# A hybrid decoder trunk: the compressed branch's second products moved behind query tiles, the Ln/Exp table load moved behind the last SiLU, and six of the last eight output tiles computed by halves of the tokens

## The chip, the cores and the metric

The kernel runs on one core of one Trainium2 chip. The metric is the device time of one execution in microseconds (us), smaller is better; it is measured for the whole program, from its start to the landing of its last output. A profiled execution gives the trace; its span runs from the first instruction to the last.

## The reference, cut to what matters

The program is a two-layer decoder trunk on 512 tokens of width 1024, in float32. Layer 0 has a recurrent mixer, layer 1 a sparse-attention mixer; each layer then has a SwiGLU feed-forward block, and a last RMSNorm makes the output. Three pieces matter here:

```python
def compress_blocks(k, pos_emb, w1, w2):
    ...
    return jax.nn.silu(flat @ w1) @ w2

def swiglu(h, w_gate_up, w_down):
    g, u = jnp.split(h @ w_gate_up, 2, axis=-1)
    return (jax.nn.silu(g) * u) @ w_down

h = h + swiglu(rmsnorm(h, ffn_norm[layer]), w_gate_up[layer], w_down[layer])
...
return rmsnorm(h, final_norm)
```

`compress_blocks` is applied to the keys and to the values of one attention branch: a first product with w1, a SiLU, and a small second product with w2 (64 by 64).

## The kernel before

**Layout.** Activations lie transposed: eight tiles of 128 features by 512 tokens (`h[0]` to `h[7]`). Each float32 operand of a product is split in a high part (a cast on ScalarE, L78) and a low part (a subtraction on VectorE, or on GpSimd for the query weights, L79), and one product takes three matmuls (L89, L90, L91). There are seven buffers for such pairs of weights (`wh`, `wl`) and three for raw weights.

**Order of the work.** The program is written as straight Python. A scheduler then orders the instructions of each engine by a simulated clock, with the order in the text as the priority; every engine runs its list in that order and waits at an instruction whose inputs are not there. An instruction with no inputs can float forward unless an edge pins it. `keep_in_program_order` pins an instruction behind the last instruction written before it on its engine. `issue_after(x)`, which the change uses more, pins what is written in its block on x's engine behind x, in the order of issue only.

**Activation tables.** ScalarE's Ln and Exp can share one table set, which L168 loads at the start and L355 is to load again at the end of each feed-forward block; SiLU (L343) has a set of its own. The toolchain inserts a load wherever the set that is active lacks the function. When it inserts loads for Ln and Exp by itself, each gets its own set.

**The odd mixer (`odd`, L703).** Four projections (L720), the row norm `row_rstd` (L735, with Ln at L127 and Exp at L128), then for each projection a tile `z` (L740). The first two go to `compress` (L825): copies into `cx` (L832), the first product (L837, eight fp32 matmuls), a SiLU made of `sigmoid` (L149: Exp, Ln, Exp) and VectorE steps that end in `u` (L850), and the second product `ps_c2` (L853 for the keys, L858 for the values). The values and gates of all tokens (`ps_v`, L755) follow, and then four query tiles (`query_tile`, L784, `AHEAD` = 4) of 24 matmuls each, before the attention loop. So in the text the second products come ahead of `ps_v` and of the query tiles. `w2` lies in the pool `oe`, which closes before the query tiles.

**The feed-forward block (`ffn`, L270).** The gate and up projections use a seven-product scheme (`product`, L290, tile `p`), the hidden tiles `hh`, `hl` (L347, L348) feed the down projection `ps_d` (L309). The row norm of the block is made in the first round, at L333. L355 stands behind the loop, but its pin goes to the last ScalarE instruction written, a weight cast of L309.

**The end (`finish`, L363).** Hidden tiles 18 to 21 are multiplied with the last weights. Output tiles 0 to 5 are made whole (L368 to L373), each squared and added to `acc`; tiles 6 and 7 by halves of the tokens (256 columns each). For each half, `pn` (L387, L389) sums the squares over the features, `rstd` (L123) makes the norm, and eight products with it (L397, L399), on VectorE and GpSimd, make the output, which goes out in four stores (L400). The first half's `acc` holds tiles 0 to 5 over all tokens.

Of the kernel before, what the change touches and what calls it, by code (L numbers as in the profile page):

```python
# [9 lines left out]
F32 = mybir.dt.float32  # L10
# [3 lines left out]
ALU = mybir.AluOpType  # L14
# [3 lines left out]
P = 128  # L18
# [16 lines left out]
BANK_OUT = (0, 3)  # L35
OWN_DOWN = (0, 3, 6)
AHEAD = 4
LEVELS = (16, 8, 4, 2, 1)
# [14 lines left out]
class Core:  # L53
# [68 lines left out]

    def rstd(self, ps, n, out):  # L123

        nc = self.nc
        t = self.sp.tile([P, T], F32, tag="tmp", name="rt", bufs=2)[:, :ps.shape[1]]
        nc.scalar.activation(t, ps, AF.Ln, bias=self.eps, scale=1.0 / n)  # L127
        nc.scalar.activation(out, t, AF.Exp, scale=-0.5)  # L128
        nc.vector.scalar_tensor_tensor(t, out, -0.5 / n, out, ALU.mult, ALU.mult)
        nc.vector.scalar_tensor_tensor(t, ps, n * EPS, t, ALU.add, ALU.mult)  # L130
        nc.vector.scalar_tensor_tensor(out, t, 1.5, out, ALU.add, ALU.mult)

# [137 lines left out]
    def ffn(self, outs, w_out, gain, layer, next_gain):  # L270
        tc, nc, io, sp = self.tc, self.nc, self.io, self.sp
        with tc.tile_pool(name="fs", bufs=1) as fs, tc.tile_pool(name="fps", bufs=6, space=PSUM) as fps:
# [44 lines left out]
            for size in GROUPS:  # L317
                hid = []
                for j in range(done, done + size):
# [22 lines left out]
                    (nc.vector if j == NF - 1 else nc.gpsimd).tensor_tensor(g, g, r, ALU.mult)  # L342
                    nc.scalar.activation(g, g, AF.Silu)  # L343
                    nc.vector.tensor_tensor(g, s, g, ALU.mult)
# [9 lines left out]
                done += size  # L354
            tc.keep_in_program_order(nc.scalar.preload_act_table_set("natural_log_exp_and_others"))  # L355
            if next_gain is None:
# [6 lines left out]
    def finish(self, hid, ws, fps):  # L363

        nc, fs, sp, h = self.nc, self.fs, self.sp, self.h
        gain = lambda m: self.par[:, C_GAIN + 32 + m:C_GAIN + 33 + m]
        acc = sp.tile([P, T], F32, tag="acc", name="acc", bufs=1)
        for m in range(KD - 2):  # L368
            ps = self.bank(m, "ps_d")
            self.dense_t(ps, self.weight(ws[m]), hid)  # L370
            nc.vector.tensor_tensor(h[m], ps, h[m], ALU.add)
            self.square(m, h[m], acc)
            nc.scalar.activation(h[m], h[m], AF.Identity, scale=gain(m))  # L373
        w = [self.weight(ws[m]) for m in (KD - 2, KD - 1)]
        for half in range(2):
            c = slice(half * TH, (half + 1) * TH)
            pn = fps.tile([P, T], F32, tag="gu", name="pn")[:, :TH]
            sqs = []
            for i in range(2):
                m = KD - 2 + i  # L380
                ps = fps.tile([P, T], F32, tag="gu", name="ps_f")[:, :TH]
                self.dense_t(ps, w[i], [(xh[:, c], xl[:, c]) for xh, xl in hid])
                nc.vector.tensor_tensor(h[m][:, c], ps, h[m][:, c], ALU.add)
                sq = fs.tile([P, TH], F32, tag="u", name="sq", bufs=4)
                nc.scalar.activation(sq, h[m][:, c], AF.Square)
                sqs.append(sq)
            nc.tensor.matmul(pn, self.ones, acc[:, c], start=True, stop=False)  # L387
            for i, sq in enumerate(sqs):
                nc.tensor.matmul(pn, self.ones, sq, start=False, stop=i == 1)  # L389
            r = fs.tile([P, TH], F32, tag="tr", name="r", bufs=7)  # L390
            self.rstd(pn, D, r)
            for i in (0, 2, 3, 1):
                o = fs.tile([P, 2, TH], F32, tag="sw" if half else ("g", "s")[i // 2], name="o", bufs=4 if half else 2)
                for j in range(2):
                    m = 2 * i + j
                    if i == 3:
                        nc.vector.scalar_tensor_tensor(o[:, j], h[m][:, c], gain(m), r, ALU.mult, ALU.mult)  # L397
                    else:
                        (nc.gpsimd if i == 2 or (i == 1 and j) else nc.vector).tensor_tensor(o[:, j], h[m][:, c], r, ALU.mult)  # L399
                nc.sync.dma_start(self.io["out"][2 * i:2 * i + 2, :, c].rearrange("m p t -> p m t"), o)  # L400
# [302 lines left out]
    def odd(self, xs, acc):  # L703
        tc, nc, io, sp = self.tc, self.nc, self.io, self.sp
        with tc.tile_pool(name="os", bufs=1) as os_, tc.tile_pool(name="ops", bufs=2, space=PSUM) as op:
# [20 lines left out]
            with tc.tile_pool(name="oe", bufs=1) as oe:  # L726
                self.oe = oe
                w1 = [oe.tile([P, 8, P], F32, tag="w1", name="w1", bufs=2) for _ in range(2)]
                w2 = oe.tile([64, 2, 64], F32, name="w2")
                for i in range(2):  # L730
# [5 lines left out]
                pss += [proj(2), proj(3)]  # L736
                rt = self.token_rstd(r, op.tile([P, T], F32, tag="po", name="ps_rt", bufs=1))
                for col, ps in enumerate(pss):
                    z = oe.tile([P, T], F32, tag="z", name="z", bufs=3)
                    nc.vector.tensor_tensor(z, ps, r, ALU.mult)  # L740
                    if col < 2:
                        self.compress(col == 1, z, w1[col], w2, kc, vc)
                    else:
                        for g in range(2):
                            self.keys(z, g, *[a[:, col - 2] for a in kk[g]])
# [27 lines left out]
            with tc.tile_pool(name="ol", bufs=1) as ol_:  # L773
# [10 lines left out]
                def query_tile(step, late=True):  # L784

                    raw = raws.popleft()
                    w = self.split(raw, WN, True)
                    query_load()
                    yield
                    ps = self.bank(0, "ps_q") if late else op.tile([P, T], F32, tag="pt", name="ps_q", bufs=3)  # L790
                    for k, (xh, xl) in enumerate(xs):
                        wh, wl = w[k // 4]
                        c = slice(k % 4 * P, k % 4 * P + P)
                        self.mm3(ps, wh[:, c], wl[:, c], xh, xl, k == 0, k == 7)
                        if k % step == step - 1:
                            yield
                    z = ol_.tile([P, T], F32, tag="qz", name="qz", bufs=9)
                    nc.vector.scalar_tensor_tensor(z, ps, 0.125, r, ALU.mult, ALU.mult)
                    qz.append(z)
                    yield  # L800

                for _ in range(2):
                    query_load()
                for _ in range(AHEAD):
                    for _ in query_tile(1, False):
                        pass
                self.attention(qz, outs, kk, kc, vt, vc, v3, gates, query_tile)
                for i, o in enumerate(outs):
# [15 lines left out]

    def compress(self, is_v, z, w1, w2, kc, vc):  # L825
        nc, os_, op = self.nc, self.os, self.op
# [12 lines left out]
        pc = os_.tile([64, 1], F32, tag="cpc", name="cpc", bufs=1)  # L839
        u = os_.tile([64, 2, 31], F32, tag="cu", name="cu", bufs=1)  # L840
        e = os_.tile([64, 2, 31], F32, tag="ce", name="ce", bufs=1)
# [7 lines left out]
        self.sigmoid(s, n, e)  # L849
        nc.vector.tensor_tensor(u, u, s, ALU.mult)  # L850
        ps2 = op.tile([P, T], F32, tag="pt", name="ps_c2", bufs=3)
        if not is_v:
# [308 lines left out]
```

## Time and profile before

| what | value |
|---|---|
| median of 3 runs | 1310.82 us (1310.17 to 1310.92) |
| the profiled execution's own time | 1311.86 us |
| its span, first to last instruction | 1308.9 us |
| TensorE busy | 1270.2 us, 97% of the span |
| TensorE's mean granted clock | 0.984 of full |
| ScalarE table loads | 21, 1.283 us each |

The profiled execution is 1.04 us above the median, and 2.96 us of its time lie outside the span. [...]

### The profile page before, as it was taken

Reading aid. Unit: us, or ns where it says so; the run is one execution under the profiler, and the core shown is the slowest. Engines: PE = TensorE matmul, PEld = TensorE weight load, DVE = VectorE, ACT = ScalarE, POOL = GpSimd, SP = SyncE. Lnnn points to the kernel's source line nnn. Section 1 sums busy time; section 2 is a strip of 40 time slices with the busy share of each in tenths; the row PEclk is TensorE's granted clock in tenths of the full one; section 3 lists DMA queues with packets and bytes.
Section 4 is the critical chain, followed back from the end, with each engine's and each line's share of the span. In section 5 each row is a group of like instructions: output and inputs, shape, how many; then the busy total and the mean of one; then the engine's idle time right before and its main releaser. Section 6 shows DMA issues by size and latency. Waiting matters only on the chain.

```text
span 1308.9 us, 21707 instructions
## 1 busy us (share of the span) xinstructions
PE 1270.2 (97%) x7846; PEld 1120.7 (86%) x7846; DVE 1028.2 (79%) x2027; ACT 731.7 (56%) x1587; POOL 332.0 (25%) x371
## 2 busy tenths in 40 slices
PE   9999999998999999999988999999989999999995
PEld 7888888888999999999877888887889999999984
DVE  7896764699998887876762789995989888878755
ACT  6655444675554444444554778895755444444444
POOL 3432431001121111111015666762012111111101
PEclk9999999999999999999997999999989999999998
DMA  7212212123233333332322211101223333333321
GB/s 262 84 65 75 72 65 65 65 81 101 85 109 109 107 106 100 100 97 88 104 90 93 78 52 52 44 18 34 85 81 125 105 97 98 97 101 102 105 57 64
DMA packets 44123, 115.10 MB, mean 88 GB/s; under 512 B 4913, under 2 KB 10481, under 8 KB 44017
## 3 DMA queue, kind: packets, MB, share of 16 engines
q1 hardware_dynamic: 43872, 113.69, 27.2%
q8 instruction: 61, 1.00, 0.3%
q14 instruction: 46, 0.37, 0.1%
q10 hardware_dynamic: 144, 0.04, 0.0%
HBM read 111.62 MB, written 2.10 MB: 87 GB/s over the span
## 4 chain that ended last, share of the span: by engine, by line
PE 60%; DVE 8%; issue 2%; DMA 2%; ACT 2%; POOL 1%; DVEq 0%; ACTq 0%; POOLq 0%
PE p L89 9%; PE p L90 9%; PE p L91 9%; PE ps_d L90 5%; PE ps_d L91 5%; PE ps_d L89 5%; DMA raw<-in_gu 2%; PE po L966 2%; PE pt L935 2%; PE ps_o L89 2%; PE ps_o L91 2%; PE ps_o L90 2%; DVE wl L79 1%; PE ps_q L89 1%; PE ps_q L90 1%
## 5 line engine op out<-in xcount | busy, mean ns | idle before, releaser
L78 ACT CAST wh<-raw 128x512 fp32r<-128x512 f32 (+2 forms) x356 | 212.8, 605 | 216.2 <-PE p L90 76.8
L79 DVE TENSOR_TENSOR wl<-raw,wh 128x512 fp32r<-128x512 f32 (+2 forms) x340 | 244.0, 723 | 43.2 <-ACT wh L78 42.1
L214 ACT CAST sh<-sw 128x512 fp32r<-128x512 f32 x176 | 107.6, 618 | 144.4 <-PE p L90 126.4
L341 POOL TENSOR_TENSOR s<-s,rstd 128x256 f32<-128x256 f32 x44 | 38.9, 884 | 510.9 <-DVE s L336 451.7
L215 DVE TENSOR_TENSOR sl<-sw,sh 128x512 fp32r<-128x512 f32 x176 | 146.3, 848 | 6.5 <-ACT sh L214 6.2
L90 PE MATMUL ps_d<-hl,wh 128*128 128x512 f32 x344 | 136.0, 395 | 0.4 <-DVE hl L348 0.2
L91 PE MATMUL ps_d<-hh,wl 128*128 128x512 f32 x344 | 135.6, 394 | 0.0
L89 PE MATMUL ps_d<-hh,wh 128*128 128x512 f32 x344 | 134.5, 396 | 0.6 <-ACT hh L347 0.5
L342 POOL TENSOR_TENSOR g<-g,rstd 128x512 f32<-128x512 f32 x42 | 70.9, 1689 | 138.2 <-DVE g L338 114.5
L259 DVE TENSOR_TENSOR sw<-raw 128x512 f32<-128x512 f32 x44 | 30.3, 689 | 65.3 <-DMA raw<-in_gu 65.2
L91 PEld LDWEIGHTS ps_d<-hh,wl 128*128 128x128 f32 x344 | 64.5, 188 | 14.9
L918 ACT ACTIVATE p<-p,mx 128x256 f32<-128x256 f32 (+3 forms) x128 | 71.6, 564 | 10.1 <-DVE mx L910 9.6
L90 PE MATMUL ps_e<-xl,wh 128*128 128x512 f32 x192 | 76.7, 401 | 0.5 <-DVE xl L109 0.5
L927 POOL TENSOR_SCALAR p<-p,sm 128x128 f32<-128x128 f32 (+3 forms) x128 | 68.6, 554 | 33.2 <-DVE sm L924 15.0
L89 PE MATMUL ps_e<-xh,wh 128*128 128x512 f32 x192 | 76.8, 403 | 0.2
L91 PE MATMUL ps_e<-xh,wl 128*128 128x512 f32 x192 | 76.6, 401 | 0.0
L90 PEld LDWEIGHTS ps_d<-hl,wh 128*128 128x128 f32 x344 | 64.7, 188 | 13.2 <-DVE hl L348 1.0
L89 PEld LDWEIGHTS ps_d<-hh,wh 128*128 128x128 f32 x344 | 64.2, 188 | 13.5 <-ACT hh L347 1.0
L910 DVE CUSTOM_DVE_ANT_0 p<-ps_s,bias 128x256 f32<-128x256 f32 (+3 forms) x128 | 59.0, 481 | 8.1 <-PE pt L935 4.9
L313 DVE TENSOR_TENSOR h<-ps_d,h 128x512 f32<-128x512 f32 x80 | 54.6, 682 | 6.5 <-PE ps_d L91 6.3
L343 ACT ACTIVATE g<-g 128x512 f32<-128x512 f32 x44 | 27.8, 632 | 53.1 <-POOL g L342 52.9
L950 DVE TENSOR_TENSOR pl<-pt,ph 128x512 fp32r<-128x512 f32 (+2 forms) x96 | 51.5, 549 | 5.9 <-ACT ph L942 5.7
(342 smaller groups left out, 4112.8 us busy)
## 6 DMA issues: line engine op xcount, KB each, us to landing
raw<-in_gu SPq DMA_DIRECT2D x88, 512.0 KB, 3.8
raw<-in_dn SPq DMA_DIRECT2D x80, 256.0 KB, 2.7
raw<-in_ein SPq DMA_DIRECT2D x22, 512.0 KB, 3.7
raw<-in_oin SPq DMA_DIRECT2D x12, 512.0 KB, 3.7
raw<-in_eout SPq DMA_DIRECT2D x8, 512.0 KB, 3.8
bias<-in_bias SPq DMA_DIRECT2D x16, 256.0 KB, 2.6
raw<-in_oout SPq DMA_DIRECT2D x8, 512.0 KB, 3.5
h<-in_x SPq DMA_DIRECT2D x8, 256.0 KB, 5.0
```

The lines of the kernel that those rows point to most:

```text
L78: nc.scalar.copy(wh[:, :m], raw[:, o:o + m])
L79: (nc.gpsimd if pool else nc.vector).tensor_tensor(wl[:, :m], raw[:, o:o + m], wh.bitcast(F32)[:, :m], ALU.subtract)
L89: mm(ps, ah, bh, start=start, stop=False, skip_group_check=more)
L90: mm(ps, ah, bl, start=False, stop=False, skip_group_check=more)
L91: return mm(ps, al, bh, start=False, stop=stop, skip_group_check=more)
L214: nc.scalar.copy(hi, src)
L215: nc.vector.tensor_tensor(lo, src, hi.bitcast(F32), ALU.subtract)
L313: nc.vector.tensor_tensor(self.h[m], ps, self.h[m], ALU.add)
L342: (nc.vector if j == NF - 1 else nc.gpsimd).tensor_tensor(g, g, r, ALU.mult)
L910: nc.vector.tensor_tensor_reduce(p, h["dst"][:, b - br[0]], h["bias"][:, T - n:], -1.0, 3e38, ALU.add, ALU.min, h["mx"][:, t, b:b + 1])
L918: nc.scalar.activation(p, p, AF.Exp, bias=h["mx"][:, t, b:b + 1], scale=-1.0, accum_out=h["sm"][:, t, b:b + 1])
L927: nc.gpsimd.tensor_scalar(p, p, h["sm"][:, t, b:b + 1], 1.0, ALU.mult, ALU.mult)
```

## The change

1. `compress` ends with `u` (two buffers now); the second products are a function of their own, `compress_out`, which is called behind the first query tile for the keys and behind the second for the values, its TensorE instructions pinned behind that tile's last matmul. `w2` moves to a pool that stays open.
2. The table load at the end of each feed-forward block is pinned behind the last SiLU as well.
3. In `finish` two output tiles are made whole and six by halves of the tokens. `acc` takes tile 6's square on VectorE, so `pn` has one product less. `pn` takes a bank of the `m0`/`m1` pair. The norm `r` is written to PSUM, ScalarE copies it to SBUF (`r2`), GpSimd makes two of the eight products of each half (it made three) and reads `r2`; VectorE makes six and reads `r` from PSUM. The stores go out in the order 0, 1, 3, 2.

```diff
+WHOLE = 2
...
-    def rstd(self, ps, n, out):
+    def rstd(self, ps, n, out, t=None, last=None):
...
-        nc.vector.scalar_tensor_tensor(out, t, 1.5, out, ALU.add, ALU.mult)
+        nc.vector.scalar_tensor_tensor(out if last is None else last, t, 1.5, out, ALU.add, ALU.mult)
...
-                    nc.scalar.activation(g, g, AF.Silu)
+                    silu = nc.scalar.activation(g, g, AF.Silu).ins
...
-            tc.keep_in_program_order(nc.scalar.preload_act_table_set("natural_log_exp_and_others"))
+            with tc.issue_after(silu):
+                tc.keep_in_program_order(nc.scalar.preload_act_table_set("natural_log_exp_and_others"))
...
-        for m in range(KD - 2):
+        for m in range(WHOLE):
...
-        w = [self.weight(ws[m]) for m in (KD - 2, KD - 1)]
+        w = {m: self.weight(ws[m]) for m in range(WHOLE, KD)}
         for half in range(2):
             c = slice(half * TH, (half + 1) * TH)
-            pn = fps.tile([P, T], F32, tag="gu", name="pn")[:, :TH]
-            sqs = []
-            for i in range(2):
-                m = KD - 2 + i
+            for m in range(WHOLE, KD):
                 ps = fps.tile([P, T], F32, tag="gu", name="ps_f")[:, :TH]
-                self.dense_t(ps, w[i], [(xh[:, c], xl[:, c]) for xh, xl in hid])
+                self.dense_t(ps, w[m], [(xh[:, c], xl[:, c]) for xh, xl in hid])
                 nc.vector.tensor_tensor(h[m][:, c], ps, h[m][:, c], ALU.add)
                 sq = fs.tile([P, TH], F32, tag="u", name="sq", bufs=4)
                 nc.scalar.activation(sq, h[m][:, c], AF.Square)
-                sqs.append(sq)
+                if m < KD - 1:
+                    nc.vector.tensor_tensor(acc[:, c], acc[:, c], sq, ALU.add)
+                if m < KD - 2:
+                    nc.scalar.activation(h[m][:, c], h[m][:, c], AF.Identity, scale=gain(m))
+            pn = self.bank(half, "pn")[:, :TH]
             nc.tensor.matmul(pn, self.ones, acc[:, c], start=True, stop=False)
-            for i, sq in enumerate(sqs):
-                nc.tensor.matmul(pn, self.ones, sq, start=False, stop=i == 1)
-            r = fs.tile([P, TH], F32, tag="tr", name="r", bufs=7)
-            self.rstd(pn, D, r)
-            for i in (0, 2, 3, 1):
+            nc.tensor.matmul(pn, self.ones, sq, start=False, stop=True)
+            r = fps.tile([P, T], F32, tag="gu", name="r")[:, :TH]
+            r2 = fs.tile([P, TH], F32, tag="tr", name="r2", bufs=7)
+            t = fs.tile([P, TH], F32, tag="tr", name="t", bufs=7)
+            self.rstd(pn, D, r2, t, r)
+            nc.scalar.copy(r2, r)
+            for i in (0, 1, 3, 2):
...
                     if i == 3:
                         nc.vector.scalar_tensor_tensor(o[:, j], h[m][:, c], gain(m), r, ALU.mult, ALU.mult)
+                    elif i == 2:
+                        nc.gpsimd.tensor_tensor(o[:, j], h[m][:, c], r2, ALU.mult)
                     else:
-                        (nc.gpsimd if i == 2 or (i == 1 and j) else nc.vector).tensor_tensor(o[:, j], h[m][:, c], r, ALU.mult)
+                        nc.vector.tensor_tensor(o[:, j], h[m][:, c], r, ALU.mult)
...
-                        self.compress(col == 1, z, w1[col], w2, kc, vc)
+                        us.append(self.compress(col == 1, z, w1[col]))
...
-                        self.mm3(ps, wh[:, c], wl[:, c], xh, xl, k == 0, k == 7)
+                        self.query_ins = self.mm3(ps, wh[:, c], wl[:, c], xh, xl, k == 0, k == 7).ins
...
-                for _ in range(AHEAD):
+                for i in range(AHEAD):
                     for _ in query_tile(1, False):
                         pass
+                    if i in (0, 1):
+                        with tc.issue_after(self.query_ins):
+                            self.compress_out(i == 1, us[i], w2, kc, vc)
```

## Rows read from the trace of the kernel before

**Rows 1.** The page's first part: busy us (share of the span) xinstructions.
```profile
PE 1270.2 (97%) x7846; PEld 1120.7 (86%) x7846; DVE 1028.2 (79%) x2027; ACT 731.7 (56%) x1587; POOL 332.0 (25%) x371
```
**Rows 2.** TensorE's waits: who waited for whom: total us, times, longest.
```profile
PE ps_c L853 <- DVE cu L850: 5.2, 1, 5.2
PE ps_c L858 <- DVE gates L767: 5.0, 1, 5.0
PE pn L387 <- DVE acc L121: 2.2, 1, 2.2
```
**Rows 3.** Stretches of odd mixer: us, busy by engine, PEclk, DMA share, GB/s.
```profile
680.84:686.04 5.20, 0.01 (x1) 0.00 (x0) 1.81 (x9) 3.63 (x6) 0.00 (x0) 0.79 0.53 202
686.04:693.28 7.24, 7.22 (x30) 6.73 (x30) 2.16 (x12) 3.41 (x11) 3.72 (x3) 0.50 0.43 145
693.28:698.25 4.97, 0.00 (x0) 0.03 (x1) 1.40 (x9) 4.88 (x10) 1.26 (x1) 0.50 0.00 2
698.25:704.30 6.05, 6.04 (x17) 4.72 (x18) 3.31 (x17) 4.59 (x9) 0.00 (x0) 0.50 0.30 89
```
**Rows 4.** VectorE and GpSimd in order of time, odd mixer: start, us, [idle before].
```profile
663.46 0.69 DVE L129 SCALAR_TENSOR_TENSOR rt<-rstd 128x512 f32<-128x512 f32 x1 [4.21 <-ACT rstd L128]
...
677.50 3.54 DVE L832 COPY cx<-z 64x256 f32<-64x256 f32 x4
...
681.22 0.46 DVE L79 TENSOR_TENSOR wl<-raw,wh 128x304 fp32r<-128x304 f32 x1
...
675.64 4.39 POOL L79 TENSOR_TENSOR wl<-raw,wh 128x512 fp32r<-128x512 f32 x3 [48.77 <-ACT wh L78]
```
**Rows 5.** Table loads and SiLU by line: ns min/median/max, first and last start.
```profile
L355 ACT ACT_TABLE_LOAD  x2: 1283/1283/1283, 598.4 to 1245.9; - x2
...
L343 ACT ACTIVATE g<-g x44: 627/632/636, 317.9 to 1270.7; 128x512 f32<-128x512 f32 x44
...
L127 ACT ACT_TABLE_LOAD  x4: 1283/1283/1283, 659.4 to 1296.9; - x4
```
**Rows 6.** Stretches at the start of both feed-forward blocks, columns as in rows 3.
```profile
944.83:956.41 11.58, 7.12 (x40) 5.54 (x38) 9.44 (x21) 7.95 (x15) 0.00 (x0) 0.87 0.19 62
956.41:960.50 4.09, 4.09 (x19) 4.09 (x20) 3.58 (x8) 1.46 (x3) 0.73 (x1) 0.52 0.43 150
296.80:308.03 11.23, 7.78 (x41) 6.22 (x39) 11.23 (x24) 6.12 (x14) 0.00 (x0) 0.85 0.11 32
```
**Rows 7.** ScalarE in order of time, last hidden tile.
```profile
1272.20 0.62 ACT L347 CAST hh<-g 128x512 fp32r<-128x512 f32 x1 [0.83 <-DVE g L344]
```
**Rows 8.** Stretches of the end, columns as in rows 3.
```profile
1287.71:1290.05 2.34, 0.17 (x2) 0.00 (x1) 1.38 (x2) 1.36 (x3) 0.00 (x0) 1.00 0.00 0
...
1291.26:1294.67 3.41, 3.41 (x18) 3.37 (x17) 0.73 (x3) 2.24 (x4) 0.00 (x0) 0.52 0.00 0
```
**Rows 9.** The chain that ended last, its end: start us, us, what.
```profile
1296.00 0.43 DVE h L383
1296.46 0.42 ACT sq L385
1296.89 1.28 ACT L127
...
1298.68 1.28 ACT L128
...
1301.79 0.43 DVE o L399
...
1303.08 1.73 DVE o L397 x2
1304.81 0.34 DVE o L399
```
**Rows 10.** TensorE in order of time: the second half's sums of squares.
```profile
1296.23 1.40 PE L389 MATMUL pn<-sq,ones 128*128 128x256 f32 x4
```
**Rows 11.** One VectorE line with a PSUM operand: ns min/median/max.
```profile
L340 DVE TENSOR_TENSOR s<-p,rstd x44: 406/412/426, 309.8 to 1270.3; 128x256 f32<-128x256 f32 x44
```

More of the change, by code (lines that the diff above doesn't have):

```diff
@@ L121, in square @@
             (nc.gpsimd if pool else nc.vector).tensor_tensor(acc, acc, sq, ALU.add)
-    def rstd(self, ps, n, out):
+    def rstd(self, ps, n, out, t=None, last=None):
         nc = self.nc
-        t = self.sp.tile([P, T], F32, tag="tmp", name="rt", bufs=2)[:, :ps.shape[1]]
+        if t is None:
+            t = self.sp.tile([P, T], F32, tag="tmp", name="rt", bufs=2)[:, :ps.shape[1]]
         nc.scalar.activation(t, ps, AF.Ln, bias=self.eps, scale=1.0 / n)
@@ L728, in odd @@
                 w1 = [oe.tile([P, 8, P], F32, tag="w1", name="w1", bufs=2) for _ in range(2)]
-                w2 = oe.tile([64, 2, 64], F32, name="w2")
+                w2 = os_.tile([64, 2, 64], F32, name="w2")
                 for i in range(2):
@@ L737, in odd @@
                 rt = self.token_rstd(r, op.tile([P, T], F32, tag="po", name="ps_rt", bufs=1))
+                us = []
                 for col, ps in enumerate(pss):
@@ L823, in keys, with compress @@
             nc.vector.tensor_tensor(kl[o], z[own], kh.bitcast(F32)[own], ALU.subtract)
-    def compress(self, is_v, z, w1, w2, kc, vc):
+    def compress(self, is_v, z, w1):
         nc, os_, op = self.nc, self.os, self.op
@@ L839, in compress @@
         pc = os_.tile([64, 1], F32, tag="cpc", name="cpc", bufs=1)
-        u = os_.tile([64, 2, 31], F32, tag="cu", name="cu", bufs=1)
+        u = os_.tile([64, 2, 31], F32, tag="cu", name="cu", bufs=2)
         e = os_.tile([64, 2, 31], F32, tag="ce", name="ce", bufs=1)
@@ L850, in compress, with compress_out @@
         nc.vector.tensor_tensor(u, u, s, ALU.mult)
+        return u
+    def compress_out(self, is_v, u, w2, kc, vc):
+        nc, os_, op = self.nc, self.os, self.op
         ps2 = op.tile([P, T], F32, tag="pt", name="ps_c2", bufs=3)
```

## The prediction

> **What bounds the kernel now.** I read the page's shares first: TensorE has a matmul in flight for 97% of the span [rows 1], so an edit pays only where TensorE stands still or runs at its lower clock. The waits of TensorE come next. Three are long: 5.2 us and 5.0 us before the second products of the compressed branch, and 2.2 us before the first half's sum of squares [rows 2]. The second of these is put down to a gates step, but what came last for it is the values' `u` (L850), behind the same SiLU chain as the keys'. Then the stretches around them show what such a wait costs beyond itself. [...] Last comes the chain from the last matmul to the last store, where two table loads and eight products stand in series [rows 9].
>
> **Second products behind query tiles.** In the odd mixer TensorE is idle for 5.20 and 4.97 us, and the 7.24 and 6.05 us of work around these waits run at half clock, so full clock would save 3.62 and 3.02 us of them [rows 3]. If the query tiles fill everything, that is 5.20 + 4.97 + 3.62 + 3.02 = 16.8 us. The moved instructions are three small matmuls (six records) and the copies out of PSUM; no DMA moves with them, and SP's queue keeps its order except that `w2` has another address. Behind the new waits stand query tiles 1 and 2; both `u` then have a whole query tile (24 matmuls) or two to get ready, and their readers, the attention steps, come after four tiles.
>
> What is late next? Three things must be there at 680.84. The last weights of `ps_v` are split at 681.22 + 0.46 = 681.68, the values' copies `cx` end at 677.50 + 3.54 = 681.04, and GpSimd's first three query splits end at 675.64 + 4.39 = 680.03 [rows 4]. So VectorE could still cost 681.68 - 680.84 = 0.84 us. But VectorE's train of work starts only at 663.46, after 4.21 us of idling for the norm [rows 4], and two table loads of 1.283 us (from 659.4 on [rows 5]) lie in that chain; without them the train is 2.57 us earlier and the splits are done before TensorE asks. Term: 15.9 to 16.8; I take **16.2**, near the upper end, because the train's own row shows the room.
>
> **Table loads.** The load of L355 runs at 598.4 and 1245.9, but the last SiLU runs at 1270.7 [rows 5], so today it is thrown away again by the next SiLU, and later Ln and Exp load their own sets by turns: 4 times at L127 alone [rows 5], and as often at L128. Pinned behind the last SiLU it holds for all Ln and Exp up to the next feed-forward block. In layer 0's mixer, where the same steps run under the set loaded at the start, no such load occurs.
>
> At the start of layer 1's feed-forward block a Ln and an Exp load go. From the norm's matmul to the seventh product's first matmul that block takes 11.58 us, and then 4.09 us at clock 0.52; layer 0's block, which has no load there, takes 11.23 us and is then at full clock [rows 6]. The like-for-like gain is 0.35 + 4.09 x 0.48 = 2.3 us. Ends: 0.3, if the clock falls all the same, and 4.5, if both loads (2.57) and the slow stretch (1.96) go; VectorE is busy for all 11.23 us in layer 0 [rows 6], so it will be the next bound. I take **2.0**.
>
> Cost of the moved load: it now sits between the last SiLU and the cast `hh`. ScalarE idles 0.83 us there [rows 7], so `hh` comes 1.28 - 0.83 = 0.45 us later. TensorE has three quarters of two tiles to do meanwhile; 0 to 0.45 us, I take **0.2**, in layer 1 alone, for in layer 0 the other tiles' products cover it.
>
> **The end by halves.** The stall of 2.34 us [rows 8] comes from the last whole tile: add, square, add, then `pn`. With halves, `pn` of half 0 waits only for a half tile's add and square, 1296.00 to 1296.89, or 0.89 us [rows 9], and the `acc` product covers a part; I leave 0.7 us standing, should the scheduler again put `pn` ahead of the next tile, and gain 1.6 (0 to 2.3). A pause so short should keep the clock up, so the 3.41 us at 0.52 [rows 8] give back 3.41 x 0.48 = 1.6 (0 to 1.6). One sum product less in half 0: two records of the 1.40 us for four [rows 10], 0 to 0.7, I take 0.4.
>
> After the last matmul, the Ln load ends at 1296.89 + 1.28 = 1298.17 [rows 9], the sum at 1296.23 + 1.40 = 1297.63 [rows 10], so 0.54 us of it are exposed; the Exp load is exposed with all 1.28 [rows 9]: 1.8, firm. The products of VectorE run from 1301.79 to 1305.15, 3.36 us for five, for two of them take 1.73 beside GpSimd [rows 9]. With the norm in PSUM I price each of the six at 0.412, the row of a product with a PSUM operand, which stays within 0.406 and 0.426 in 44 calls spread over the feed-forward blocks [rows 11]: 2.5 us. ScalarE's copy for GpSimd runs beside them. That saves 0.9; as four stores then come closer together, I take 0.6 (0 to 0.9). A norm written to PSUM by VectorE has no row; by the nearest, reading from PSUM, it costs nothing either way.
>
> [...]
>
> Sum of the end: 1.6 + 1.6 + 0.4 + 1.8 + 0.6 = **6.0** (1.8 to 7.3).
>
> **Sum.** 16.2 + 2.0 + 6.0 - 0.2 = 24.0 us. The profiled execution took 1311.86 us, so 1287.9; it stands 1.04 above the median of the runs, so the median should come to 1311.86 - 24.0 - 1.04 = **1286.8 us**. All lows, 15.9 + 0.3 + 1.8 - 0.45 = 17.6, give 1293.3; all highs, 16.8 + 4.5 + 7.3 = 28.6, give 1282.2. A run of this kernel can tell a change of about 0.2%, 2.6 us, from none.
>
> **Rivals.**
> *One wait comes back in the odd mixer.* The query tiles need casts from ScalarE and splits from GpSimd for each half tile of weights; if a tile waits for them as long as TensorE waited for the values, 4.97 + 3.02 = 8.0 us of the gain go: 1294.8. For it: these engines run their lists in order, with the SiLU chain ahead. Against: three of eight halves are split before 680.03 [rows 4], and the chain loses its loads. Chance 0.13.
> *The end stalls as before.* `pn` goes ahead of half 1's tiles, stalls as long, and the clock falls: 3.2 us of the 6.0 go, 1290.0. For it: that order stands in the list now. Chance 0.10.
> *The load doesn't hold*, being placed elsewhere or followed by loads the toolchain inserts again: 2.0 + 1.8 + 0.8 less the 0.2 go, 1291.2. Against: no load in layer 0's mixer. Chance 0.06.
> *A switch costs more than its row.* If ScalarE needed as long again after a load before its next step, the four exposed loads would each give back 1.28 us more: 5.1 in all, 1281.7. In the chain the square ends at 1296.88, the Exp load stands between 1298.68 and 1299.96, and its user follows at once [rows 9]: no room. Chance 0.02. [...]
> *Slower: VectorE paces the twelve half tiles.* Each gives VectorE an add into `h` and most an add into `acc`, and TensorE needs some 0.1 us for each of a half tile's 12 matmuls (18 in 3.41 us at 0.52 [rows 8]), 1.2 us. If TensorE waited w in each and fell to the lower clock, 144 matmuls would take 0.09 us more each, 13.1, and 12 w beside. Against the other gains of 20.8 it is slower by over 2.6 us from w = 0.86 on; at w = 1.1 it gives 1316.3. Two adds of 0.41 [rows 11] leave room below 1.2, so VectorE would have to be over a microsecond behind in every one. Chance 0.03, of which 0.01 falls within 0.2%.
>
> **How the numbers follow.** The forecast has 0.66. The range reaches from near all highs, 1283, over the end's stall and the lost load to just past the wait that comes back, 1296; outside are the slow case, the longer switch and the worse half of that wait, some 0.13. Every case but the slow one is faster by over 0.2%: 0.97 faster, 0.01 same, 0.02 slower.
>
> **What would show it.** Right: no wait of TensorE over 1 us between the first `ps_v` matmul and the last query tile, and clock 1.00 there; five table loads in place of 21 (one at the start, and per layer one for SiLU and one behind it); no load in the last chain; products of VectorE near 0.41 us at the end. The steps part at these places: a wait before a `ps_q` matmul is the first rival, idle time before `pn` followed by clock 0.5 the second, loads at L127 the third. The forecast is wrong if TensorE's idle time turns up elsewhere, above all at the start of the attention steps, or if those prove to be bound by another engine.

## The result, and the profile after

The median went from 1310.79 us (four runs) to 1294.47 us (four runs, 1292.59 to 1296.57); the ratio is 0.9877 [0.986, 0.9894]. The forecast was 1286.8 us with a range of 1283 to 1296. The profiled execution is the shortest of the four: 1292.59 us, with a span of 1290.7 us against 1308.9 us before; as the one before lay above its median and this one lies below, the two spans differ by 18.2 us, the medians by 16.3. The sign was right, and so was the mechanism of the largest term, the second products. The size was 16.3 us where 24.0 were forecast, and most of what is missing is missing at the end.

The page's first part of the kernel after [rows 1]:

```profile
PE 1260.3 (98%) x7890; PEld 1113.5 (86%) x7890; DVE 1037.3 (80%) x2039; ACT 713.5 (55%) x1581; POOL 331.4 (26%) x369
```

TensorE's waits after (total us, times, longest) [rows 2]:

```profile
PE pn L392 <- DVE acc L388: 5.0, 2, 3.1
PE p L90 <- ACT u L332: 1.7, 2, 0.9
PE ps_c L852 <- DVE cx L848: 1.7, 1, 1.7
PE p L90 <- ACT u L337: 1.6, 2, 0.9
PE p L90 <- DVE g L333: 1.6, 2, 1.0
```

Both waits of 5 us for the second products are gone. One of 1.7 us for the copies `cx` is new, and the wait before `pn`, 2.2 us once, is now 5.0 us in two pieces, although the change was to remove it. The table loads by line:

```profile
L345 ACT ACT_TABLE_LOAD x2 | 2.6, 1283 | 0.0
L358 ACT ACT_TABLE_LOAD x2 | 2.6, 1283 | 0.0
...
L170 ACT ACT_TABLE_LOAD x1 | 1.3, 1283 | 0.7 <-PEq L1171 0.7
```

Five are left, as forecast: one at the start, and per layer one for SiLU and one behind it.

To see where the time went I cut both traces at four instructions that both kernels have: the norm's sum product of each block and the last SiLU of each layer. Starts are read from the two timelines, the ends of the spans to 0.1 us:

| stretch | before, us | after, us | gained | forecast |
|---|---|---|---|---|
| start to layer 0's feed-forward norm | 296.80 | 297.49 | -0.7 | - |
| to its last SiLU (623.24, 622.67) | 326.44 | 325.18 | 1.3 | - |
| to the odd mixer's norm (658.34, 658.00) | 35.10 | 35.33 | -0.2 | - |
| to layer 1's feed-forward norm (944.83, 929.38) | 286.49 | 271.38 | **15.1** | 16.2 |
| to the last SiLU (1270.75, 1253.97) | 325.92 | 324.59 | **1.3** | 2.0 |
| to the end of the span (1308.9, 1290.7) | 38.15 | 36.73 | **1.4** | 6.0 |

They add up to the spans' difference, 18.2 us. The forecast's remaining term, a loss of 0.2 for the delayed `hh`, would fall into the last line, but TensorE has no wait for `hh` behind the last SiLU. The 1.3 us in layer 0's feed-forward block are no gain of the change, which alters nothing there before the last SiLU: in the second trace of the same kernel, below, this block took 326.92 us, more than before.

**The odd mixer** after (us, busy by engine, PEclk, DMA share, GB/s) [rows 3], then VectorE and GpSimd there in order of time [rows 4]:

```profile
664.74:679.13 14.39, 12.70 (x96) 12.28 (x94) 13.99 (x26) 7.82 (x14) 3.99 (x3) 1.00 0.23 75
679.13:684.84 5.71, 5.71 (x45) 5.71 (x43) 3.52 (x10) 3.41 (x11) 2.24 (x2) 1.00 0.74 245
684.84:708.68 23.84, 23.84 (x106) 18.70 (x105) 16.31 (x34) 9.57 (x25) 18.11 (x16) 1.00 0.37 120
```
```profile
665.13 1.56 DVE L847 COPY cx<-z 64x256 f32<-64x256 f32 x4
...
672.83 4.56 DVE L847 COPY cx<-z 64x256 f32<-64x256 f32 x4
...
672.69 4.08 POOL L80 TENSOR_TENSOR wl<-raw,wh 128x512 fp32r<-128x512 f32 x3 [45.91 <-ACT wh L79]
```

The granted clock is 1.00, full speed, throughout, and from 679.13 us on TensorE never stands still. The first stretch lacks 1.69 us: the keys' four copies took 1.56 us, the values' same four took 4.56 us while GpSimd split weights, so that these copies came last. So one of the prediction's signs of being right, no wait over 1 us behind the first `ps_v` matmul, did not come.

**The end** after: VectorE in order of time, then TensorE's sums of squares.

```profile
1269.60 0.42 DVE L131 SCALAR_TENSOR_TENSOR t<-r 128x256 f32<-128x256 f32 x1 [2.18 <-ACT r L130]
...
1271.44 1.42 DVE L409 TENSOR_TENSOR o<-h,r 128x256 f32<-128x256 f32 x4 [0.49 <-ACT r L399]
1272.78 0.86 DVE L405 SCALAR_TENSOR_TENSOR o<-h,par,r 128x256 f32<-128x256 f32 x2
1273.56 0.42 DVE L384 TENSOR_TENSOR h<-ps_f,h 128x256 f32<-128x256 f32 x1
1274.46 0.43 DVE L388 TENSOR_TENSOR acc<-acc,sq 128x256 f32<-128x256 f32 x1 [0.48 <-ACT sq L386]
...
1279.77 0.41 DVE L384 TENSOR_TENSOR h<-ps_f,h 128x256 f32<-128x256 f32 x1
```
```profile
1267.47 0.70 PE L392 MATMUL pn<-acc,ones 128*128 128x256 f32 x2 [1.91 <-DVE acc L388]
...
1279.91 0.70 PE L392 MATMUL pn<-acc,ones 128*128 128x256 f32 x2 [3.13 <-DVE acc L388]
```

TensorE is through with half 1's tiles at 1276.8 us. But VectorE's list has half 0's norm and its six products in front of half 1's first add, which so starts at 1273.56 us; by then TensorE is through with more than three of half 1's six tiles (they begin at 1268.25 and take 1.36 us each). From there add, ScalarE's square and add into `acc` follow one another at 1.24 us per tile, and TensorE waits 3.13 us for the last of them. The theory that I took into the experiments: **at the end the order of VectorE's list is the bound, not the half tiles.**

### The profile page after: what moved, and what is told of

It is laid out like the page before. It is cut to its first block, busy times and chain, and to the rows that moved or that the text cites. A ratio compares the mean times of both kernels' runs of the same rounds, so it can differ in the third digit from the quotient of the medians.

```text
span 1290.7 us, 21806 instructions
## 1 busy us (share of the span) xinstructions
PE 1260.3 (98%) x7890; PEld 1113.5 (86%) x7890; DVE 1037.3 (80%) x2039; ACT 713.5 (55%) x1581; POOL 331.4 (26%) x369
## 4 chain that ended last, share of the span: by engine, by line
PE 74%; DVE 15%; DMA 4%; issue 3%; ACT 2%; POOL 1%; SPq 0%; DVEq 0%; POOLq 0%; ACTq 0%
PE p L90 8%; PE p L91 8%; PE p L92 8%; PE ps_d L91 4%; PE ps_d L92 4%; PE ps_d L90 4%; DMA raw<-in_gu 4%; PE ps_e L90 3%; PE ps_e L91 3%; PE ps_e L92 3%; PE ps_o L90 3%; PE ps_o L91 3%; PE ps_o L92 3%; DVE wl L80 3%; PE po L985 2%
## 5 line engine op out<-in xcount | busy, mean ns | idle before, releaser
L91 PE MATMUL ps_d<-hl,wh 128*128 128x512 f32 x328 | 129.7, 395 | 0.3 <-DVE hl L350 0.2
L92 PE MATMUL ps_d<-hh,wl 128*128 128x512 f32 x328 | 129.3, 394 | 0.0
L90 PE MATMUL ps_d<-hh,wh 128*128 128x512 f32 x328 | 128.5, 396 | 0.8 <-ACT hh L349 0.8
L92 PEld LDWEIGHTS ps_d<-hh,wl 128*128 128x128 f32 x328 | 61.5, 188 | 14.2
L91 PEld LDWEIGHTS ps_d<-hl,wh 128*128 128x128 f32 x328 | 61.7, 188 | 12.4 <-DVE hl L350 0.9
L90 PEld LDWEIGHTS ps_d<-hh,wh 128*128 128x128 f32 x328 | 61.2, 188 | 12.9 <-ACT hh L349 1.0
```

The costliest lines, as they stand in the source:

```text
L90: mm(ps, ah, bh, start=start, stop=False, skip_group_check=more)
L91: mm(ps, ah, bl, start=False, stop=False, skip_group_check=more)
L92: return mm(ps, al, bh, start=False, stop=stop, skip_group_check=more)
```

## The experiments

The medians carry about 2 us of their own, for which the last experiments find a reason only in part, so parts are also compared by the stretches of the table.

**The change as it is, again.**

> The change as it is, as the yardstick for the parts: 1294.5 us by its first runs, a gain of 16.3. If the trace of its fastest run is typical, some 15 of it arise in the odd mixer, 1.3 at the start of layer 1's feed-forward block and 1.4 behind the last SiLU. If the spread of 4 us between its first runs belongs to the kernel and not to the chip, it appears here again, and the longer runs show a lower clock.

1294.58 us (1292.6 to 1295.62), ratio 0.9877 [0.9863, 0.989]. In its trace the odd mixer's stretch took 271.33 us, the last one 37.57 us (0.8 more than in the first trace: around half 0's sum, behind the same wait of 1.91 us, the clock fell to 0.50 for 3.4 us). The longest of these four runs has the highest mean clock, 0.993, so here the clock does not explain the spread.

The three gains that the change aims at repeat within a microsecond (15.2, 2.3 and 0.6 us here), but the odd mixer's sum hides something: behind the same wait of 1.69 us for `cx` the clock, which stayed at 1.00 in the first trace, fell here (columns as in rows 3).

```profile
681.10:684.50 3.40, 3.40 (x15) 3.40 (x15) 2.12 (x6) 1.54 (x7) 1.29 (x1) 0.51 0.87 306
```

The first `ps_cs` matmul so came 52.2 us behind the norm's product where the first trace has 50.7, and the rest of the stretch was as much shorter; why is open.

**The second products alone** (`compress` split in two, `compress_out` behind the query tiles; the rest as before).

> Only the second products behind the query tiles; the table loads and the end stay as before. Theory (the parts share the odd mixer): the two loads in front of VectorE's train there hold the copies cx back by 2.57 us, and TensorE, which in the whole change waits 1.7 us for them, waits some 4.3; gain 15.2 - 2.6 = 12.6, so 1298.2 us. Rival (the parts add up, as the prediction has it): the loads cost nothing once the second products wait behind query tiles, gain 15.2, 1295.6 us.

1303.47 us, 0.9941 [0.9928, 0.9953]. The odd mixer's stretch took 275.45 us, 11.0 less than before, so both expectations are too high, the theory by 1.6, the rival by 4.2. TensorE's waits in that stretch:

```profile
PE ps_c L842 <- DVE cx L838: 3.6, 1, 3.6
```

As the theory has it, the wait for `cx` is longer (3.6 where the whole change has 1.7), since ScalarE still loads two tables (1.28 us each) ahead of VectorE's train. Behind this wait the clock is at 0.50 from 681.9 to 688.7 us, which neither expectation had. The median gained 6.9, the profiled execution, one of the two shortest, 2.4 more; layer 0's block, which this part does not touch, took 1.3 us longer in it than before and holds one wait of TensorE of 1.8 us for `s`.

**The table load alone.**

```diff
-                    nc.scalar.activation(g, g, AF.Silu)
+                    silu = nc.scalar.activation(g, g, AF.Silu).ins
...
-            tc.keep_in_program_order(nc.scalar.preload_act_table_set("natural_log_exp_and_others"))
+            with tc.issue_after(silu):
+                tc.keep_in_program_order(nc.scalar.preload_act_table_set("natural_log_exp_and_others"))
```

> Only the table load behind the last SiLU; the second products and the end stay as before. Theory (the parts share the odd mixer): each of the two sigmoid chains that TensorE waits for holds a Ln and an Exp load (2.57 us), and the norm ahead of them another two, so the first wait of 5.2 us goes with its slow stretch (5.2 + 3.6) and the second shrinks by 2.6; with 1.3 at the feed-forward block and 1.8 in the last chain the gain is 14.5, 1296.3 us. Rival (the parts add up): only the 1.3 and the 1.8 come, gain 3.1, 1307.7 us.

1300.56 us, 0.9921 [0.9907, 0.9934]. The odd mixer's stretch took 276.08 us, 10.4 less than before (theory 11.4, rival 0), the last stretch 35.88 us, 2.3 less. Layer 1's feed-forward block, where 1.3 were expected, took 326.09 us, 0.2 more than before, although its start is 1.2 us shorter (below). TensorE's waits in the odd mixer:

```profile
PE ps_c L859 <- DVE gates L768: 4.2, 1, 4.2
PE ps_c L854 <- DVE cu L851: 1.3, 1, 1.3
```

The first wait shrank from 5.2 to 1.3, because the sigmoid in front of it no longer loads two tables (1.28 us each before), and from 682 to 690 us the clock stays at 1.00; only at the second wait it still falls, to 0.50 from 691.5 to 698.3 us. So the first two parts of the change share the odd mixer: alone they gain 11.0 and 10.4 there, together 15.1. My sum had given all 16.2 to one of them and told of the loads only as room for it.

**The halves alone** (the new `finish` and `rstd`; loads as before).

> Only the end by halves; the last chains of Ln and Exp load their tables as before, now for both halves. Theory (VectorE's list is the bound: half 0's norm and six products stand ahead of half 1's adds, which then go in series with ScalarE's squares): half 0's norm comes 2.57 us later for its loads and half 1's adds with it, so instead of a gain there is a loss of up to 2.2 us (2.57 less the 0.4 that the halves gave without loads), 1310.8 to 1313.0 us. Rival (the prediction's terms): stall 1.6 + clock 1.6 + sum product 0.4 + products 0.6 = 4.2 us gained, 1306.6 us.

1312.26 us, 1.0012 [1.0003, 1.0021]; the last stretch took 39.25 us, 1.1 more than before. The rival, which is my prediction's sum, is out: without the loads' removal the halves make the end longer. They do so with it too: the last stretch took 35.88 us with the load pinned alone and 36.73 and 37.57 us in the two traces of the whole change. So in the change as it is, all of the gain at the end comes from the loads, and the halves cost about a microsecond. TensorE's waits there with the halves alone:

```profile
PE pn L391 <- DVE acc L387: 5.8, 2, 4.4
```

**Half 0's products behind half 1's adds** (on top of the whole change: the norm stays in its place, its readers are written after the loop over half 1's tiles).

```diff
...
+                with tc.issue_after(add):
+                    products(0, *r0)
...
```

> The whole change, but half 0's output products are issued on VectorE behind the last add of half 1, instead of ahead of half 1's adds; the norm of half 0 stays where it is. The measure is the stretch from the last SiLU to the end of the span: 36.7 and 37.6 us in two traces of the change. Theory (VectorE's list is the bound): half 1's adds start at once behind half 0's norm and keep pace with TensorE, which ends half 1's tiles 8.4 us after its sum products; the six products fall into the 2.3 us in which VectorE idles before half 1's norm; TensorE's wait of 3.1 us before half 1's sum of squares falls to about 0.6, the stretch is 2.5 us shorter (34.2 to 35.1). Rival (half tiles as such are too slow: add, square, add in series): adds stay at 1.24 us per tile behind TensorE, the six products only move to the end, and the stretch stays within 0.5 us of 36.7 to 37.6.

The stretch took 34.22 us: 2.5 less than in the first trace of the change, 3.4 less than in the second, as the theory has it (1293.7 us as a whole, 0.9871 [0.9851, 0.9891]; in this trace layer 0's block took 329.24 us, with the clock at 0.50 for 6.8 us of it). The rows that answer to those above:

```profile
1271.57 0.42 DVE L411 TENSOR_TENSOR h<-ps_f,h 128x256 f32<-128x256 f32 x1
1272.47 0.75 DVE L415 TENSOR_TENSOR acc<-acc,sq 128x256 f32<-128x256 f32 x1 [0.48 <-ACT sq L413]
...
1278.12 0.42 DVE L411 TENSOR_TENSOR h<-ps_f,h 128x256 f32<-128x256 f32 x1
1278.45 1.40 DVE L403 TENSOR_TENSOR o<-h,r 128x256 f32<-128x256 f32 x4
1279.78 0.86 DVE L399 SCALAR_TENSOR_TENSOR o<-h,par,r 128x256 f32<-128x256 f32 x2
```
```profile
1278.26 0.70 PE L383 MATMUL pn<-acc,ones 128*128 128x256 f32 x2 [0.76 <-DVE acc L415]
```

The add follows half 0's norm at once, the products stand where VectorE had been idle, and the wait of 3.13 us is 0.76. The chain per tile is still 1.24 us (1276.88 to 1278.12 for the last one); it never was too slow for TensorE, which needs 1.36 us for a half tile of twelve matmuls (0.113 us apart). It only started too late.

**Half 0's norm behind half 1's first tile too.**

```diff
...
+                if half and m == WHOLE + 0:
+                    with tc.issue_after(mm):
+                        r0 = norm(0, sq0)
...
```

> As the kernel with the late products, and half 0's sum of squares and norm are also issued behind half 1's first tile on TensorE. Theory (list order): TensorE's wait of 1.9 us before half 0's sum goes too, since a tile of 1.36 us stands between; the stretch from the last SiLU to the end is 4.5 us shorter than in the change, 32.2 to 33.1 us, and the whole kernel at 1290.0 us by medians. Rival (the squares bind): half 0's last square and add come later than one tile, 0.5 us of the wait stay, and half 1's first add waits behind half 0's norm; 3 us shorter.

The stretch took 33.29 us, 0.2 outside the theory's 32.2 to 33.1; 1289.76 us as a whole, 0.9841 [0.9821, 0.9862]. Of the wait of 1.91 us before half 0's sum, 0.85 stays: one tile in between covers about half of it, so the rival's reason has a share as well.

**The values' copies on ScalarE** (on top of the whole change).

```diff
-                nc.vector.tensor_copy(x[par * 64:(par + 1) * 64, :, g * 32:(g + 1) * 32], src)
+                (nc.scalar.copy if is_v else nc.vector.tensor_copy)(x[par * 64:(par + 1) * 64, :, g * 32:(g + 1) * 32], src)
```

> The whole change, but the values' four copies cx are made by ScalarE instead of VectorE. The measure is the stretch from the odd mixer's norm product to the first ps_cs, 50.7 and 52.2 us in two traces of the change. Theory (VectorE's copies run beside GpSimd's query splits, 1.14 us each where they take 0.39 alone, and TensorE waits 1.7 us for them): ScalarE is free from 671.6 us on, four copies take about 0.4 each there, cx is ready 3 us earlier and the wait goes; 1.7 us shorter. Rival (a wait takes its place): TensorE next needs the last ps_v weights, split by VectorE at 678.4, and waits for these instead; under 0.5 us shorter.

From the odd mixer's norm product to the first `ps_cs` it took 48.73 us, 1.95 less than in the first trace of the change and 3.5 less than in the second, and no wait of TensorE over 0.25 us is left there; 1289.57 us as a whole, 0.9853 [0.9833, 0.9872]. ScalarE's copies:

```profile
670.71 2.60 ACT L847 COPY cx<-z 64x256 f32<-64x256 f32 x4
```

They take 0.65 us each, not the 0.4 that I had expected, but end at 673.31 instead of 677.39 us. GpSimd's splits begin later here, at 674.39 us, behind casts of ScalarE that now follow the copies, so this run separates the two engines in time and does not show how ScalarE's copies fare beside such splits. VectorE's small steps of the keys' SiLU meet the splits instead, three of them at 1.19 to 1.25 us each where they took 0.19 to 0.21, without a wait of TensorE.

The copies' wait bears on the clock too. Four traces hold it at 1.69 us: two of the change, and the ones with the late products and with the late norm. In two of the four the clock is at 0.50 for 3.4 us behind it (the second of the change, and the late norm), in the other two it stays at 1.00. In all six traces with the copies on ScalarE, here and below, the wait is gone and the clock stays at 1.00 there.

**Both together.**

> The late products, the late norm and the copies on ScalarE together: if both theories hold and the parts add up, 4.5 + 1.7 = 6.2 us faster than the change, 1288.3 us by medians; if the rivals hold in both places, 1291.5 us.

1287.68 us (1283.9 to 1293.04), 0.9828 [0.9803, 0.9852]: 6.9 us below the change's 1294.58, about the sum of the two expectations; last stretch 33.34 us, first `ps_cs` after 48.73 us. By the intervals this version can be told from the change; the late products alone and the copies alone can't, and the late norm hardly, so these rest on the stretches. The five runs lie 9 us apart, and the shorter ones have the higher mean clock, which asked for the next two.

**The same once more, and with the waits filled.** 

> The best version so far once more, as yardstick for the two others: 1287.7 us by its first runs, which lay between 1283.9 and 1293.0, the shorter ones at the higher mean clock (0.998 and 0.991). If the clock at the starts of the feed-forward blocks makes the spread, a run whose clock stays at 1.00 there comes out near 1284, one with a fall in both blocks near 1290 or above.

1285.95 us (1284.16 to 1286.44), 0.9814 [0.9797, 0.9831], mean clocks 0.995 to 0.997. Layer 1's feed-forward block, 6 to 16 us behind its norm product, in the traces of the first and the second series (columns as in rows 3):

```profile
931.90:941.90 10.00, 8.30 (x67) 8.09 (x68) 9.11 (x19) 5.23 (x11) 1.55 (x2) 1.00 0.36 120
```
```profile
932.37:942.37 10.00, 8.43 (x46) 8.14 (x47) 7.98 (x15) 4.05 (x9) 0.73 (x1) 0.66 0.36 120
```

One and the same kernel, and waits of 0.7, 1.0 and 0.9 us in front in both: once the clock stays at 1.00, once it falls to 0.50 at 933.8 us. That block, from norm to last SiLU, took 322.76 and 324.88 us in the two. Layer 0's block took 324.25 and 326.62 us, with the clock at 1.00 in both, so as much again of the difference is not the clock's.

The first attempt to fill these waits with unused matmuls also pinned products behind them:

> The best version, with six unused matmuls (0.12 us each) in front of each of the four products at which TensorE idles at the start of a feed-forward block (0.7 to 1.0 us each); 24 per block, their sums are read by nobody. Theory (it is these idle times that let the clock fall, in some executions and not in others): the clock stays at 1.00 behind both norms in the trace and in every run, the runs lie within 2 us of 1284.5, the mean clock at 0.997 or above. Rival (the clock falls by chance whatever TensorE does there): the runs spread from 1284 to 1293 as before, and the fillers that are not hidden add up to 1 us.

1300.28 us, 0.9929 [0.9912, 0.9946], far worse than either expected. It tells nothing of the clock: the pins kept products from running early, as they do otherwise, and TensorE waited 5.4 us for `s` and 3.7 us for a cast remainder. The second attempt leaves the products' order there nearly as it was; `fill` is called three times at the start of each block:

```diff
+            def fill(after):
+                ps = self.bank(0, "ps_w")[:, :TH]
+                with tc.issue_after(after):
+                    for _ in range(FILL):
+                        f = nc.tensor.matmul(ps, a[1][0][:, :P], b[1][0][0], start=True, stop=True).ins
+                return f
```

> The best version with the products' order on TensorE left as it is, and six unused matmuls (0.12 us each) in three of the four idle times of each feed-forward block's start: 36 in all, read by nobody. They are queued behind the matmul before the wait, and 0.69 us of them fit into 0.87 us or more of waiting, so they cost next to nothing themselves. Theory (these idle times let the clock fall, in some executions and not in others): clock 1.00 behind both norms in the trace, mean clock 0.997 or above in every run, all runs within 1.5 us of 1284.5. Rival (the falls come by chance, whatever TensorE does in these waits): runs between 1284 and 1290 or more with mean clocks down to 0.993, as the two series of the best version had them.

1285.06 us (1284.25 to 1287.94), 0.98 [0.9775, 0.9824]. The mean clocks are as the theory has them: 0.997 or 0.998 in all five runs, where the ten runs of the two series without fillers have 0.991 to 0.998 and six of them lie below 0.997. In the one trace the clock is 1.00 behind both norms. That the fillers did it is not shown: this series ran on another chip than the two others, and the next experiment, without fillers, has 0.997 and 0.998 in three of four runs and 1.00 behind both norms in its trace. The times follow only in part: two runs lie above 1286, so at most some of the spread is the clock, and what moves the rest is open. Nor are the fillers a gain that these runs could show: in the trace the two feed-forward blocks took 326.71 and 324.22 us, 2.5 and 1.5 more than in the first trace without fillers, whose clock stayed at 1.00 as well.

**The norm of each half in SBUF only.**

```diff
-            r = fps.tile([P, T], F32, tag="gu", name="r")[:, :TH]
...
-            self.rstd(pn, D, r2, t, r)
-            nc.scalar.copy(r2, r)
-            return r, r2
+            self.rstd(pn, D, r2, t, r2)
+            return r2, r2
```

> The best version, with the norm of each half written to SBUF only, read there by VectorE's and GpSimd's products; no copy by ScalarE. It measures what the norm in PSUM is worth. The stretch from the last VectorE step of half 1's norm to the end of VectorE's products is 3.1 us now (0.43 norm, 0.49 waiting for ScalarE's copy, 2.2 for six products). Theory (GpSimd slows VectorE's products from SBUF, as in the kernel before, where two beside GpSimd took 1.73 us): four products beside GpSimd's two take 0.87 each, two 0.43, 4.2 us in all with the copy's wait gone, so 1 us longer. Rival (the wait for the copy is all that the norm in PSUM brings, products as fast from SBUF): 2.7 us, 0.5 us shorter.

From the start of the norm's last step to VectorE's last product it took 3.73 us, 0.6 more than the 3.13 of the best version; the theory's sign, at little more than half its size, for only two of the four products without a gain met GpSimd's (0.94 us each; the other two took 0.43 and 0.41):

```profile
1273.68 0.42 DVE L134 SCALAR_TENSOR_TENSOR r<-t,r 128x256 f32<-128x256 f32 x1
1274.14 2.48 DVE L402 TENSOR_TENSOR o<-h,r 128x256 f32<-128x256 f32 x4
1276.54 0.87 DVE L398 SCALAR_TENSOR_TENSOR o<-h,par,r 128x256 f32<-128x256 f32 x2
```

Yet the whole last stretch is 0.7 us shorter (32.62), for without the copy the scheduler interleaves half 0's norm with half 1's adds in VectorE's list, half 1's last add starts 20.81 instead of 22.48 us after the last SiLU, and TensorE's waits before `pn`, 0.85 and 0.87 us in the second series of the best version, are gone. 1283.53 us, 0.9803 [0.9786, 0.982], the shortest median of all; its interval overlaps those of the two versions next to it, so the three can't be told apart, but all three are faster than the change (0.9877 [0.9863, 0.989]).

## Why the prediction was right, and where it was not

**What bounds it: right up to the last matmul.** The large gain is TensorE's two waits and the stretches at a clock of 0.50 behind them [rows 3]. At the end the gain lies behind the last matmul, where two loads went from the chain. Of the prediction's signs of being right, the five loads, no load in the last chain and products near 0.41 us came; no wait over 1 us and a clock of 1.00 in the odd mixer did not, for 1.69 us of waiting stood there in both traces of the change and the clock fell behind it in the second.

**Second products, 16.2 forecast, 15.1 measured.** Both long waits and both slow stretches went; the 1.1 us missing is the wait for `cx`. I had read the row that says so, four copies in 3.54 us beside GpSimd's splits [rows 4], and let 2.57 us of earlier start outweigh it. The copies moved up by 4.67 us and GpSimd's splits by 2.95 us, so that three copies met a split where two had, and they took 4.56 us. This is the first rival in small: a wait came back, of 1.7 us and not of the 8.0 that I had priced, and for VectorE instead of the query tiles' casts.

**Table loads, 2.0 forecast at layer 1's block, 1.3 measured** (2.3 in the second trace, -0.2 with the load pinned alone), **and by another way than forecast.** The two loads went. From the norm product to the seventh product's first matmul layer 1's block now takes 10.26 us where it took 11.58, and layer 0's 9.98 where it took 11.23; after, in the columns of rows 6:

```profile
929.38:939.64 10.26, 7.01 (x40) 5.62 (x38) 9.31 (x20) 5.43 (x13) 0.00 (x0) 0.84 0.24 76
936.40:943.20 6.80, 6.03 (x28) 5.74 (x28) 5.71 (x11) 2.40 (x5) 0.73 (x1) 0.50 0.51 176
297.49:307.47 9.98, 6.22 (x41) 4.93 (x39) 9.98 (x21) 6.18 (x14) 0.00 (x0) 1.00 0.12 33
```

I had priced the loads at 0.35 us, by layer 0's 11.23, and the clock at 1.96 us. The clock fell all the same, for 6.8 us, and gave nothing; the loads gave 1.3. Layer 0 was no like for like: its 11.23 us hold 3.4 us at the lower clock, the 0.85 in rows 6, which I read over; at full clock it takes 9.98. So the term came close by two errors that offset each other. That the loads cost time here is shown: in three traces that keep them (before, the second products alone, the halves alone) layer 1's start takes 10.88 to 11.93 us, in the nine traces without loads and fillers 9.14 to 10.38. The whole block varies by more than that from trace to trace, so its own 1.3 and -0.2 do not measure it. What is next is open: VectorE is busy for 9.31 of the 10.26 us, as the prediction said, but of TensorE's four waits there two end with a step of VectorE and two with a copy of ScalarE. The rival that the load doesn't hold is out.

**The end, 6.0 forecast, 1.4 measured: here the prediction failed, in its first term.** I let the stall of 2.34 us shrink to 0.7. It became 1.91 + 3.13 = 5.04, so that term is -2.7 where I had +1.6. The others came near the forecast: the clock stayed at 1.00 up to the last sum (1.6), one sum product less in half 0 (0.4), two loads out of the last chain (1.8); only the products and stores gave 0.3 instead of 0.6, for the first product waits 0.49 us for ScalarE's copy. -2.7 + 1.6 + 0.4 + 1.8 + 0.3 = 1.4, what the stretch shows. The 1.6 for the clock was luck in part. I had given it for a pause of 0.7 us; that so short a pause keeps the clock up was an estimate of mine. In the trace before, the clock stays at 1.00 behind a pause of 0.80 us that ends at 113.90 and falls to 0.50 right behind one of 0.79 us that ends at 301.44. Behind the 1.91 us that came it stayed up in the first trace and fell for 3.4 us in the second. Without the 1.8 the sum is -0.4, a loss, as the runs with the loads alone and the halves alone have it too. The step that failed is that I asked what half 0's `pn` waits for and never wrote down VectorE's list for two halves: norm and products of the first stand in front of the adds of the second. The rival that the end stalls as before, to which I gave 0.10, has the right place with another cause; the slower rival, VectorE pacing every half tile, is out by its price: 1.24 us per tile against TensorE's 1.36. Reordering that list took 2.5 us off the stretch, and the norm behind the next tile another 0.9.

The six products from PSUM cost what I took: four in 1.42 us and two in 0.86 us, undisturbed by GpSimd. Reading the norm from PSUM made them no dearer here than from SBUF: the two with a gain took 0.86 us from PSUM in the change and 0.87 us from SBUF in the last experiment. What the norm in PSUM does bring is that VectorE's products are as fast beside GpSimd's as alone: those without a gain took 0.41 to 0.42 us each in the change, and 0.94 with the norm in SBUF where GpSimd ran beside them.

## What to carry to other kernels

Before work is cut into halves, write each engine's list for both halves one under the other: what closes the first half must not stand in front of what the second half's producer waits for, and the idle time before the second closing is the place for it. Where two edits shorten the same chain, price them together and each alone; here 11.0 and 10.4 us made 15.1. A copy that took 0.39 us each in one row and 0.89 in another is not one price: look at the single durations and at which neighbour ran beside each, and separate the two. When an edit pulls work forward on one engine, ask how far its neighbour's work moves with it.

## What the runs showed of the hardware that was not expected

VectorE's copies `cx` took 0.37 to 0.39 us each alone, and 1.36 to 1.39 us beside one of GpSimd's splits (of 1.3 to 1.7 us). The means of 0.89 and 1.14 us that the prediction and the experiments go by mix the two: two of the values' four copies met a split before, three after. Nanoseconds min/median/max of these four, before and after:

```profile
L832 DVE COPY cx<-z x4: 371/876/1377, 677.5 to 680.7; 64x256 f32<-64x256 f32 x4
L847 DVE COPY cx<-z x4: 375/1374/1393, 672.8 to 677.0; 64x256 f32<-64x256 f32 x4
```

Each of the five that met a split began while one ran and ended 0.23 to 0.24 us behind the end of that split. What holds the copy so long no run here shows.

The first product of a half waits 0.49 us for ScalarE's copy of the norm, though it needs nothing from it: both only read one PSUM tile. In the trace of the change the copy (0.37 us, at 1271.04 and 1283.92) is what ends the wait, in both halves, and VectorE's first product begins 0.03 and 0.04 us behind it. So here a norm in PSUM was read by the two engines one after the other; why, no run here shows.

And behind equal waits of TensorE of at most 1.0 us the granted clock stayed at 1.00 in some executions of a kernel and fell to 0.50 in others, and so it did behind equal waits of 1.69 and of 1.91 us. What decides it no run here shows.
